# A hybrid decoder layer on one core: the up projection's products reordered, a w_out tile by its other half, embedding products in both pools, triangular products merged

## The chip, the cores and the metric

The kernel runs on one core of one Trainium2 chip. The metric is the device time of one execution in microseconds (us). A time "of a kernel" is the median over several executions; a profile is of one execution, whose own time is given beside it. TensorE is called PE here and its weight loads PEld; VectorE is DVE, ScalarE is ACT, GpSimd is POOL, SyncE is SP.

## The reference

One decoder layer on x of 512 tokens by 1024 features, all in fp32. Cut to the parts that the change touches:

```python
# stick-breaking attention, per head: s < t
z = einsum('bhqd,bhkd->bhqk', qi, kt) * scale
log_keep = where(before, log_sigmoid(-z), 0)
later = cumsum(log_keep, axis=3, reverse=True) - log_keep
a = where(before, exp(log_sigmoid(z) + later), 0)
...
merged = g0 * (o_da @ w_branch_da) + g1 * (o_sb @ w_branch_sb) + g2 * (o_dl @ w_branch_dil)
x = layer_norm(ALPHA * x + merged @ w_out)
...
h = square(relu(x @ w_up))                        # 1024 -> 4096
x = layer_norm(ALPHA * x + h @ w_down + sigmoid(x @ w_g) * (p @ w_ple))
```

The remaining parts (input projection, differential and dilated attention, the three branch projections) are the same in both kernels.

## The kernel before

**Precision.** Each fp32 operand is split into a rounded part and a remainder ("h" and "l": `wh`, `wl`, `x1hT`, `x1lT`, `mh`, `ml`). A product is then three matmuls that add into one bank of the accumulator memory (PSUM): h by h, h by l, l by h. Lines L87 to L89 (`mm3`) are these three for the input projection and the up projection; L887 to L889 are the three of w_out, L955 to L957 those of the embedding, L1017 to L1019 those of its gate. ACT makes the rounded part of a weight chunk (cast at L243, 128x1024), DVE the remainder (L245, `wl<-raw,wh`).

**PSUM.** There are eight banks of 128x512, in two pools that each hand out their banks in rotation: `mm_bank` has two, `at_bank` six. A bank is handed out again only when the readers of its previous content are done.

**Items.** From the input projection on, the program is a list of items. Each names the weight chunks that it needs, a bank, a function `mm` that issues the products and a function `ev` that issues the evacuation (the copy or sum that reads the bank); `ev` of an item is called just before `mm` of the next. An item with no bank of its own takes one of `mm_bank`. Weight chunks are loaded by SP's queue (`raw`), in the order in which `chunk` was called, and cast in the same order, a ring ahead of the items that use them. Sums of weight blocks (`usum`, `dsum`) are made ahead of time by accumulating transfers on POOL's queue. The order of the calls is not altogether the order on an engine: some products of a neighbouring item are moved forward or back when the program is built.

**Stages**, by the first and last weight load in the trace: the heads of the stick-breaking attention put their triangular products (L1666) between other work from 29.7 to 217.9 us; w_out (`wout_items`) runs from 607.4 to 657.3, the embedding (`ple_items`) from 658.0, its gate (`pleg_items`, L1017) from 672.2 to 709.5, and the MLP from there to the end.

**Up projection.** The 4096 hidden features are in eight blocks `m`. A block is 2x2 halves of the weights by 2x2 quarters of x and is computed in Strassen's manner, with seven block products instead of eight; `forms[p]` are the needed sums of quarters of x. A block has two tiles `j` of 128 features each, and a tile four parts, so the items of a block run a0, a1, b0, b1, c0, c1, e0, e1 (`up_parts`, `pair`). Every product here is 128x256, and a block product of a tile is four steps of three matmuls, so 12 of them. Part a has two block products: the one with weight quarter "12", which is called the *second product* below, into the upper half (`HC`) of a bank, and the one with "11", the *first product*, into the lower half (`HB`). Between them ACT copies the second product out to a tile `up` (L1195). The first product remains in the bank, which parts b, c and e use on. Part a's `ev` adds the lower half and the copy into `hid`. L1229 is the last reader of the bank, in part e.

From block 1 on the items of the down projection (`down_parts`, L1261 to L1263, 128x512) of the block before are put between those of up parts, a fixed share after each up part from the third on in a stage; stages hold blocks 0; 1 and 2; 3 and 4; 5 and 6; 7.

**w_out.** Output tile `tt` (four of them, times two halves of the columns) sums eight k steps over `merged_T`, the transposed and split merged rows. `turn_item` makes these: eight transposes (L794), ACT's rounding to `mh` (L798), DVE's remainder `ml`. In the first half of the columns, two turn items follow tile 0 and two more tile 1; those behind tile 1 make k steps 0 to 3 of tiles 2 and 3, those behind tile 0 their k steps 4 to 7.

**Embedding.** Eight products p·w_ple of 6 matmuls each, in `at_bank`; ACT copies each to a tile `ple` (L961). Between them stand the transposes of the normalised rows (L924, `ln1_gen`), in `at_bank` as well, whose readers are ACT's `x1hT` and `x1r` (L937) and DVE's `x1lT` (L931).

**Triangular products.** Per head, the suffix sums within a key block are products of `tri_r` with the split log terms `sph` and `spl`. Key blocks 2 and 3 are two halves of one bank (number 2, 256 columns each), and their terms are two halves of one tile.

Of the kernel before, what the change touches and what calls it, by code (L numbers as in the profile page):

```python
# [55 lines left out]
def trunk(tc, a, out):  # L56
    nc = tc.nc
    es = ExitStack()
    with es:
# [14 lines left out]
        def slot(name, dt=F32):  # L74
            return big.tile([P, 512], dt, name=nm(name), tag="s", bufs=NSLOT)
# [4 lines left out]
        def mm_bank():  # L80
            return psum.tile([P, 512], F32, name=nm("mm"), tag="mm", bufs=2)
# [184 lines left out]
        def item(cs, mm, ev, need=None, bank=None, size=1.0):  # L266
            items.append({"c": cs, "mm": mm, "ev": ev, "need": need, "bank": bank, "size": size})
# [93 lines left out]
        HB = slice(0, 256)  # L361
        HC = slice(256, 512)
# [514 lines left out]
        def wout_items():  # L877
            for half in range(2):
                cs = [chunk(a["wo"][half, c].rearrange("p k n -> p (k n)"), 1024) for c in range(4)]
                for tt in range(4):  # L880
                    def mm(ps, tt=tt, cs=cs):
                        for k in range(8):
                            c = cs[k // 2]
                            s = slice((k % 2) * 512, (k % 2) * 512 + 512)
                            h, lo = merged_T[k // 4, tt // 2, k % 4 // 2]
                            q = slice(k % 2 * 256 + tt % 2 * P, k % 2 * 256 + tt % 2 * P + P)
                            nc.tensor.matmul(ps, h[:, q], c["h"][:, s], start=k == 0, stop=False)  # L887
                            nc.tensor.matmul(ps, h[:, q], c["l"][:, s], start=False, stop=False)
                            nc.tensor.matmul(ps, lo[:, q], c["h"][:, s], start=False, stop=k == 7)  # L889

                    def ev(ps, tt=tt, half=half):
                        y = xn.pop((tt, half))
                        if not half:
                            x1sum[tt] = small("lsm", 2)
                        i = nc.vector.scalar_tensor_tensor(y, y, ALPHA, ps, op0=OP.mult, op1=OP.add,
                                                           accum_out=x1sum[tt][:, half:half + 1])
                        st["added"] = getattr(i, "ins", i)
                        x1[tt, half] = y
                        if half:
                            pending.append(ln1_gen(tt))  # L900
                    item(cs if tt == 3 else [], mm, ev, need=cs, bank=at_bank)
                    for t in {0: [(1, 1, 0), (1, 1, 1)], 1: [(0, 1, 0), (0, 1, 1)]}.get(tt, ()) if not half else ():
                        turn_item(*t)
# [41 lines left out]
        def ple_items():  # L945
            cs = [chunk(a["wp"][half].rearrange("p k n -> p (k n)"), 1024) for half in range(2)]
            for half in range(2):
                for tt in range(4):
                    def mm(ps, tt=tt, half=half):
                        c = cs[half]  # L950
                        for k in range(2):
                            s = slice(k * 512, k * 512 + 512)
                            q = slice(tt * P, tt * P + P)
                            h, lo = pTs[k]
                            nc.tensor.matmul(ps, h[:, q], c["h"][:, s], start=k == 0, stop=False)  # L955
                            nc.tensor.matmul(ps, h[:, q], c["l"][:, s], start=False, stop=False)
                            nc.tensor.matmul(ps, lo[:, q], c["h"][:, s], start=False, stop=k == 1)  # L957

                    def ev(ps, tt=tt, half=half):
                        t = slot("ple")  # L960
                        nc.scalar.copy(t, ps)  # L961
                        ple[tt, half] = t
                    item([cs[half]] if tt == 3 else [], mm, ev, need=cs, bank=at_bank)


        sums_first = set()
# [158 lines left out]
        hid = {}  # L1125
# [33 lines left out]
        def up_parts(m):  # L1159

            cs = {}
            wu = a["wu"][m]

            def operand(n):
                src = usum[m][n] if isinstance(n, int) else wu[{"11": 0, "12": 1, "21": 2, "22": 3}[n]].rearrange(
                    "p k n -> p (k n)")
                cs[n] = chunk(src, 1024)

            def pair(j):
                js = slice(256 * j, 256 * j + 256)  # L1170
                b = {}

                def prod(ps, p, n, start, stop):
                    c = cs[n]
                    for k in range(4):
                        s = slice(512 * j + k * P, 512 * j + k * P + P)
                        mm3(ps, c["h"][:, s], c["l"][:, s], *forms[p][k], start and k == 0, stop and k == 3)

                def bank(n, new):
                    def f():  # L1180
                        b[n] = new()
                        return b[n]
                    return f

                def add(need, mm, ev, bank):
                    if j == 0:
                        for n in need:
                            operand(n)
                    item([cs[n] for n in need] if j else [], mm, ev, need=[cs[n] for n in need], bank=bank)

                def part_a():
                    def mm(ps):
                        prod(ps[:, HC], 2, "12", True, True)
                        b["s"] = slot("up")
                        nc.scalar.copy(b["s"][:, HB], ps[:, HC])  # L1195
                        prod(ps[:, HB], 1, "11", True, False)

                    def ev(ps):
                        if j == 0:
                            hid[m] = [slot("hid") for _ in range(4)]  # L1200
                        nc.vector.tensor_add(hid[m][0][:, js], ps[:, HB], b["s"][:, HB])
                    add(("12", "11"), mm, ev, bank("x", mm_bank))

                def part_b():
                    def mm(ps):
                        prod(ps[:, HB], 7, 2, True, False)
                        prod(b["x"][:, HB], 6, 1, False, False)

                    def ev(ps):
                        nc.scalar.copy(b["s"][:, HC], b["x"][:, HB])  # L1210
                        nc.scalar.copy(b["s"][:, HB], ps[:, HB])
                    add((2, 1), mm, ev, bank("y", at_bank))

                def part_c():
                    def mm(ps):
                        prod(ps[:, HB], 5, 0, False, False)

                    def ev(ps):
                        nc.vector.tensor_add(hid[m][3][:, js], ps[:, HB], b["s"][:, HB])
                    add((0,), mm, ev, lambda: b["x"])  # L1220

                def part_e():
                    def mm(ps):
                        prod(b["x"][:, HB], 3, 3, False, True)
                        prod(ps[:, HB], 4, "22", False, True)

                    def ev(ps):
                        nc.vector.tensor_add(hid[m][1][:, js], ps[:, HB], b["s"][:, HC])
                        nc.scalar.activation(hid[m][2][:, js], b["x"][:, HB], AF.Relu)  # L1229
                        if j:  # L1230
                            for n, sign in ((0, 1.0), (2, 0.0), (1, -1.0), (3, -1.0)):
                                if sign:
                                    nc.scalar.activation(hid[m][n], hid[m][n], AF.Relu, scale=sign)
                                nc.scalar.activation(hid[m][n], hid[m][n], AF.Square)
                    add((3, "22"), mm, ev, lambda: b["y"])
                return [part_a, part_b, part_c, part_e]
            return [x for y in zip(pair(0), pair(1)) for x in y]

# [218 lines left out]
        tri_r = one.tile([P, P], F32R, name="tri_r")  # L1457
# [151 lines left out]
        def sb_head(hd):  # L1609
# [5 lines left out]
            bank = [at_bank() for _ in range(3)]  # L1615
            for kb, bi, c0, n in reversed(blk):
                m = mask_b.rearrange("p a b -> p (a b)") if kb == 3 else mask_b[:, 1, :]
# [43 lines left out]
                yield  # L1661
            ah, al = {}, {}
            for kb, bi, c0, n in reversed(blk):
                ps = bank[bi][:, c0:c0 + n]
                for hl in (sph, spl):
                    nc.tensor.matmul(ps, tri_r, hl[bi][:, c0:c0 + n], start=False, stop=False, skip_group_check=True)  # L1666
                if kb < 3:
                    n2, hl = later[kb]
                    for t in hl:
# [488 lines left out]
```

## Time and profile before

| | |
|---|---|
| median of 3 runs | 1039.94 us (1039.53 to 1040.59) |
| profiled execution, its own time | 1040.08 us |
| its span, first to last instruction | 1038.1 us |
| mean granted clock of PE | 0.998 |
| instructions | 15050 |
| DMA moved | 249.21 MB, mean 240 GB/s |

The span is what the rows of the trace cover; the execution's own time is 2.0 us longer. In rows of the trace the first column is the start in us from the span's beginning (or a window), the second the time that the row's instructions took, then engine, line, operation, output and inputs; "x8" stands for eight in a row that were folded together. A bracket at the end is the time for which the engine was idle before it, and what ended that. A line's number is that of the kernel before.

### The profile page before, as it was taken

To read this page: it belongs to the slowest core of one execution; us is meant where nothing else is said; L and a number is where in the kernel's file an instruction comes from. 1 tells how busy PE (TensorE), PEld (TensorE's weight loads), DVE (VectorE), ACT (ScalarE), POOL (GpSimd) and SP (SyncE) were. 2 spreads that over 40 slices of the span, in tenths; PEclk is the share of its full clock that TensorE was granted. 3 is DMA by queue.
4 is the path that set the end of the run, shared out by engine and by line. 5 is a ranking of instruction groups with operands and counts; after the bars stand their busy time and mean duration, and the time that the engine had idled before them with its cause. 6 is when DMAs were issued, how large, how long until landed. Compare 5 with 4: busy or idle time off the path is not lost.

```text
span 1038.1 us, 15050 instructions
## 1 busy us (share of the span) xinstructions
PE 1028.0 (99%) x5448; PEld 881.2 (85%) x5448; DVE 787.0 (76%) x1412; ACT 591.7 (57%) x1010; POOL 180.1 (17%) x271
## 2 busy tenths in 40 slices
PE   9999999999999999999999999999999999999997
PEld 6888888889888888888888888889999889889886
DVE  6888667769765657779688885798768877877965
ACT  7566544536434645676675743775666556555651
POOL 0002411120211232411011040111111111111001
PEclk9999999999999999999999999999999999999999
DMA  8449968485976999977789795579999999998612
GB/s 309 121 156 271 277 193 217 120 290 144 285 182 222 271 272 294 238 205 199 227 269 235 267 320 182 160 222 319 331 290 315 301 306 340 303 295 279 235 57 81
DMA packets 71322, 249.21 MB, mean 240 GB/s; under 512 B 8808, under 2 KB 9592, under 8 KB 71248
## 3 DMA queue, kind: packets, MB, share of 16 engines
q0 software_dynamic: 32464, 116.21, 44.8%
q1 hardware_dynamic: 38208, 131.13, 35.1%
q8 instruction: 43, 0.70, 0.3%
q10 hardware_dynamic: 576, 0.92, 0.2%
q14 instruction: 31, 0.25, 0.1%
HBM read 246.10 MB, written 98.59 MB: 332 GB/s over the span
## 4 chain that ended last, share of the span: by engine, by line
PE 94%; DVE 2%; ACT 1%; DMA 1%; issue 1%; SPq 0%; POOL 0%; DVEq 0%; ACTq 0%; POOLq 0%
PE mm L87 10%; PE mm L88 10%; PE mm L89 10%; PE at L1261 4%; PE at L1262 4%; PE at L1263 4%; PE at L599 3%; PE at L600 3%; PE at L601 3%; PE mm L496 2%; PE mm L498 2%; PE mm L497 2%; PE at L89 1%; PE at L88 1%; PE at L87 1%; PE at L761 1%
## 5 line engine op out<-in xcount | busy, mean ns | idle before, releaser
L243 ACT CAST wh<-raw 128x1024 fp32r<-128x1024 f32 x257 | 268.6, 1049 | 242.0 <-PE mm L88 134.2
L245 DVE TENSOR_TENSOR wl<-raw,wh 128x1024 fp32r<-128x1024 f32 x257 | 312.7, 1223 | 112.9 <-ACT wh L243 111.3
L87 PE MATMUL mm<-xhT,wh 128*128 128x512 f32 x302 | 119.1, 394 | 0.0
L89 PE MATMUL mm<-xhT,wl 128*128 128x512 f32 x302 | 118.2, 391 | 0.0
L88 PE MATMUL mm<-xlT,wh 128*128 128x512 f32 x302 | 118.1, 391 | 0.0
L1261 PE MATMUL at<-wh,hh 128*128 128x512 f32 x188 | 73.7, 392 | 0.0
L87 PE MATMUL mm<-x1hT,wh 128*128 128x256 f32 x256 | 73.7, 288 | 0.0
L1262 PE MATMUL at<-wl,hh 128*128 128x512 f32 x188 | 73.7, 392 | 0.0
L1263 PE MATMUL at<-wh,hl 128*128 128x512 f32 x188 | 73.1, 389 | 0.0
L88 PE MATMUL mm<-x1lT,wh 128*128 128x256 f32 x256 | 72.2, 283 | 0.0
L89 PE MATMUL mm<-x1hT,wl 128*128 128x256 f32 x256 | 71.8, 283 | 0.0
L89 PEld LDWEIGHTS mm<-xhT,wl 128*128 128x128 f32 x302 | 56.8, 188 | 11.9
L87 PEld LDWEIGHTS mm<-xhT,wh 128*128 128x128 f32 x302 | 56.7, 188 | 11.0
L88 PEld LDWEIGHTS mm<-xlT,wh 128*128 128x128 f32 x302 | 56.7, 188 | 10.8
L87 PEld LDWEIGHTS mm<-x1hT,wh 128*128 128x128 f32 x256 | 48.7, 190 | 4.8 <-ACT up L1195 3.0
L88 PEld LDWEIGHTS mm<-x1lT,wh 128*128 128x128 f32 x256 | 48.8, 191 | 1.5
L89 PEld LDWEIGHTS mm<-x1hT,wl 128*128 128x128 f32 x256 | 48.6, 191 | 0.0
L1095 POOL DMA_DIRECT2D usum<-in_wu_dram x32 | 28.3, 921 | 101.6 <-DMA usum<-usum 34.8
L1095 POOL DMA_DIRECT2D dsum<-in_wd_dram x28 | 25.6, 936 | 102.5 <-DMA dsum<-dsum 37.0
L1263 PEld LDWEIGHTS at<-wh,hl 128*128 128x128 f32 x188 | 35.3, 188 | 7.7
L1261 PEld LDWEIGHTS at<-wh,hh 128*128 128x128 f32 x188 | 35.5, 189 | 6.0
L1262 PEld LDWEIGHTS at<-wl,hh 128*128 128x128 f32 x188 | 35.5, 189 | 5.5
(601 smaller groups left out, 2677.2 us busy)
## 6 DMA issues: line engine op xcount, KB each, us to landing
usum<-in_wu_dram POOLq DMA_DIRECT2D x48, 512.0 KB, 9.0
dsum<-in_wd_dram POOLq DMA_DIRECT2D x42, 512.0 KB, 8.9
raw<-in_wt_dram SPq DMA_DIRECT2D x38, 512.0 KB, 5.1
raw<-usum SPq DMA_DIRECT2D x32, 512.0 KB, 7.7
raw<-dsum SPq DMA_DIRECT2D x28, 512.0 KB, 7.0
raw<-in_wd_dram SPq DMA_DIRECT2D x25, 512.0 KB, 6.1
raw<-in_wu_dram SPq DMA_DIRECT2D x24, 512.0 KB, 7.6
raw<-in_wv_dram SPq DMA_DIRECT2D x18, 512.0 KB, 5.7
```

The costliest lines, as they stand in the source:

```text
L87: nc.tensor.matmul(ps, wh, xh, start=start, stop=False, skip_group_check=True)
L88: nc.tensor.matmul(ps, wh, xl, start=False, stop=False, skip_group_check=True)
L89: nc.tensor.matmul(ps, wl, xh, start=False, stop=stop, skip_group_check=True)
L243: i = nc.scalar.copy(h, raw)
L245: i = nc.vector.tensor_sub(lo, raw, h.bitcast(F32))
L599: nc.tensor.matmul(ps, h[:, q], c["h"][:, n], start=go, stop=False, skip_group_check=True)
L600: nc.tensor.matmul(ps, h[:, q], c["l"][:, n], start=False, stop=False, skip_group_check=True)
L601: nc.tensor.matmul(ps, lo[:, q], c["h"][:, n], start=False, stop=end, skip_group_check=True)
L1095: i = nc.gpsimd.dma_start(o, i, accum_op=OP.add, max_dma_last_dim=4096)
L1261: nc.tensor.matmul(ps, h[:, q], c["h"][:, s], start=go, stop=False, skip_group_check=True)
L1262: nc.tensor.matmul(ps, h[:, q], c["l"][:, s], start=False, stop=False, skip_group_check=True)
L1263: nc.tensor.matmul(ps, lo[:, q], c["h"][:, s], start=False, stop=end, skip_group_check=True)
```

## The change

It has four parts.

**1. Up projection, part a.** The two tiles of a block keep their items a0 and a1, but a0 now issues the second products ("12") of both tiles, each into the upper half of its own `mm_bank` bank and each followed by its copy, and a1 the first products ("11") of both, with the add into `hid` of tile 0 between them and that of tile 1 as its `ev`. Chunk "11" is asked for in a1 instead of a0, so behind the chunks of a down item that stands between the two.

```diff
 def pair(j):
     js = slice(256 * j, 256 * j + 256)
-    b = {}
+    b = both[j]
...
 def part_a():
+    def first(i):
+        nc.vector.tensor_add(hid[m][0][:, 256 * i:256 * i + 256], both[i]["x"][:, HB],
+                             both[i]["s"][:, HB])
+
     def mm(ps):
-        prod(ps[:, HC], 2, "12", True, True)
-        b["s"] = slot("up")
-        nc.scalar.copy(b["s"][:, HB], ps[:, HC])
-        prod(ps[:, HB], 1, "11", True, False)
+        for i in range(2):
+            if j == 0:
+                if i:
+                    both[i]["x"] = mm_bank()
+                x, k = both[i]["x"], "12"
+                prod(x[:, HC], 2, k, True, True, i)
+                both[i]["s"] = slot("up")
+                nc.scalar.copy(both[i]["s"][:, HB], x[:, HC])
+            else:
+                prod(both[i]["x"][:, HB], 1, "11", True, False, i)
+                if not i:
+                    first(i)
 
     def ev(ps):
         if j == 0:
             hid[m] = [slot("hid") for _ in range(4)]
-        nc.vector.tensor_add(hid[m][0][:, js], ps[:, HB], b["s"][:, HB])
-    add(("12", "11"), mm, ev, bank("x", mm_bank))
+        else:
+            first(1)
+    operand(("12", "11")[j])
+    need = [cs[("12", "11")[j]]]
+    item(need, mm, ev, need=need, bank=(lambda: b["x"]) if j else bank("x", mm_bank))
```

PE at part a of block 0. Before, tile 0 is bank `mm_6921` and tile 1 `mm_6955`; `wh_6820` is chunk "12" and `wh_6826` chunk "11":

```order
L87 MATMUL mm_6921<-x1hT,wh_6820 128x256 [waits Activation_49]
...
L89 MATMUL mm_6921<-x1hT,wl_6821 128x256
L87 MATMUL mm_6955<-x1hT,wh_6820 128x256
...
L87 MATMUL mm_6955<-x1hT,wh_6820 128x256
L87 MATMUL mm_6921<-x1hT,wh_6826 128x256 [waits Activation_49]
...
L89 MATMUL mm_6921<-x1hT,wl_6827 128x256
L88 MATMUL mm_6955<-x1lT,wh_6820 128x256
```

The same place after, where tile 0 is `mm_6905`, tile 1 `mm_6920`, chunk "12" `wh_6804` and chunk "11" `wh_6810`:

```order
L87 MATMUL mm_6905<-x1hT,wh_6804 128x256 [waits Activation_49]
...
L89 MATMUL mm_6905<-x1hT,wl_6805 128x256
L87 MATMUL mm_6920<-x1hT,wh_6804 128x256
...
L89 MATMUL mm_6920<-x1hT,wl_6805 128x256
L87 MATMUL mm_6905<-x1hT,wh_6810 128x256 [waits Activation_49]
...
L89 MATMUL mm_6905<-x1hT,wl_6811 128x256
L87 MATMUL mm_6920<-x1hT,wh_6810 128x256 [waits Activation_49]
```

Before, four products of tile 1 stood between tile 0's second and first product; now all 12 do, and tile 1's first product stands behind the 12 of tile 0's.

ACT around the two copies of the last block, before:

```order
L243 CAST wh_9530<-raw_9390 128x1024 [waits DMAHW1_49,PE_49]
L1195 COPY up_9558<-mm_9545 128x256 [waits PE_49]
L243 CAST wh_9604<-raw_9411 128x1024 [waits DMAHW2_49,PE_49]
L1195 COPY up_9590<-mm_9577 128x256 [waits PE_49]
L243 CAST wh_9610<-raw_9417 128x1024 [waits DMAHW3_49,PE_49]
L1211 COPY up_9558<-at_9617 128x256 [waits DVE_49,PE_49]
```

and after:

```order
L243 CAST wh_9514<-raw_9374 128x1024 [waits DMAHW1_49,PE_49]
L1208 COPY up_9542<-mm_9529 128x256 [waits PE_49]
L243 CAST wh_9559<-raw_9395 128x1024 [waits DMAHW2_49,PE_49]
L1208 COPY up_9557<-mm_9544 128x256 [waits PE_49]
L243 CAST wh_9594<-raw_9401 128x1024 [waits DMAHW3_49,PE_49]
L1252 ACTIVATE hid_9565<-hid_9565 128x512 [waits DVE_49]
```

The copies (L1208 is L1195 of before) have a cast between them in both; behind them part b's copy has moved behind the work on `hid`.

**2. w_out.** The third tile of the first half of the columns takes its k steps in the order 4 to 7, 0 to 3.

```diff
+ks = (4, 5, 6, 7, 0, 1, 2, 3) if tt == 2 and not half else range(8)
+
-def mm(ps, tt=tt, cs=cs):
-    for k in range(8):
+def mm(ps, tt=tt, cs=cs, ks=ks):
+    for k in ks:
...
-        nc.tensor.matmul(ps, h[:, q], c["h"][:, s], start=k == 0, stop=False)
+        nc.tensor.matmul(ps, h[:, q], c["h"][:, s], start=k == ks[0], stop=False)
         nc.tensor.matmul(ps, h[:, q], c["l"][:, s], start=False, stop=False)
-        nc.tensor.matmul(ps, lo[:, q], c["h"][:, s], start=False, stop=k == 7)
+        nc.tensor.matmul(ps, lo[:, q], c["h"][:, s], start=False, stop=k == ks[-1])
```

**3. Embedding.** In the first half of the columns, tiles 1 and 3 take a bank of `mm_bank`.

```diff
-item([cs[half]] if tt == 3 else [], mm, ev, need=cs, bank=at_bank)
+item([cs[half]] if tt == 3 else [], mm, ev, need=cs,
+     bank=None if tt % 2 and not half else at_bank)
```

PE's first product of tiles 1 to 3 and of the fifth tile, and the transposes of the next token tile (L924 before, L926 after); before:

```order
L955 MATMUL at_6448<-wh_6217,pTh_6255 128x512 [waits DVE_49,Activation_49]
...
L955 MATMUL at_6469<-wh_6217,pTh_6255 128x512 [waits DVE_49,Activation_49]
...
L955 MATMUL at_6490<-wh_6217,pTh_6255 128x512 [waits DVE_49]
...
L955 MATMUL at_6505<-wh_6223,pTh_6255 128x512 [waits Activation_49]
...
L924 MATMUL at_6514<-ident,xn_5943 128x128 [waits DVE_49,Activation_49]
```

and after:

```order
L957 MATMUL mm_6432<-wh_6201,pTh_6239 128x512 [waits PE_49]
...
L957 MATMUL at_6453<-wh_6201,pTh_6239 128x512 [waits DVE_49,Activation_49]
...
L957 MATMUL mm_6474<-wh_6201,pTh_6239 128x512
...
L957 MATMUL at_6489<-wh_6207,pTh_6239 128x512 [waits DVE_49,Activation_49]
...
L926 MATMUL at_6498<-ident,xn_5927 128x128 [waits DVE_49]
```

Every tile is where it was in the row; two of them no longer take a turn in the rotation of six, so the fifth takes another bank of it.

**4. Triangular products.** The products of key block 2 are left out, and those of key block 3 run over the whole bank: two of 512 columns for four of 256.

```diff
 for kb, bi, c0, n in reversed(blk):
     ps = bank[bi][:, c0:c0 + n]
-    for hl in (sph, spl):
-        nc.tensor.matmul(ps, tri_r, hl[bi][:, c0:c0 + n], start=False, stop=False, skip_group_check=True)
+    for hl in (sph, spl) if kb != 2 else ():
+        nc.tensor.matmul(bank[bi][:, :w[bi]], tri_r, hl[bi], start=False, stop=False,
+                         skip_group_check=True)
```

The rest of the program is unchanged. The order of POOL's instructions is the same; on SP's queue only loads of the MLP change places, as said under part 1.

More of the change, by code (lines that the diff above doesn't have):

```diff
@@ L1161, in up_parts @@
             cs = {}
+            both = [{}, {}]
             wu = a["wu"][m]
@@ L1170, in pair, with prod @@
                 js = slice(256 * j, 256 * j + 256)
-                b = {}
-                def prod(ps, p, n, start, stop):
+                b = both[j]
+                def prod(ps, p, n, start, stop, j=j):
                     c = cs[n]
@@ L1663, in sb_head @@
             for kb, bi, c0, n in reversed(blk):
-                ps = bank[bi][:, c0:c0 + n]
-                for hl in (sph, spl):
-                    nc.tensor.matmul(ps, tri_r, hl[bi][:, c0:c0 + n], start=False, stop=False, skip_group_check=True)
+                for hl in (sph, spl) if kb != 2 else ():
+                    nc.tensor.matmul(bank[bi][:, :w[bi]], tri_r, hl[bi], start=False, stop=False,
+                                     skip_group_check=True)
                 if kb < 3:
```

## The prediction

> **What bounds the kernel now.** I read the busy table first, then the chain of waits, then who waited for whom on PE's weight loads (PEld). Matmuls are pipelined, so a stalled PE still shows as busy; the start times of successive weight loads show a stall better.
>
> ```profile
> PE 1028.0 (99%) x5448; PEld 881.2 (85%) x5448; DVE 787.0 (76%) x1412; ACT 591.7 (57%) x1010; POOL 180.1 (17%) x271
> PE 94%; DVE 2%; ACT 1%; DMA 1%; issue 1%; SPq 0%; POOL 0%; DVEq 0%; ACTq 0%; POOLq 0%
> PEld mm L87 <- ACT up L1195: 3.0, 13, 0.3
> PEld at L955 <- ACT ple L961: 0.6, 1, 0.6
> PEld at L887 <- ACT mh L798: 0.5, 1, 0.5
> ```
>
> PE is the bound from end to end: 99% busy and 94% of the chain. So only two things help: PE waits that disappear, or PE work that disappears. Three of the few waits PE has are where this change edits: the copy of a second product in the up projection (3.0 us in 13 pieces), one embedding product (0.6) and the third w_out tile (0.5). That is a ceiling of 4.1 us, and what an idle time is worth has to be read from the loads around it.
>
> **Up projection, what one wait costs.** Part a computes a tile's second product into the upper half of a bank, ACT copies it out (L1195), and the first product goes into the lower half of the same bank. PE waits for the copy. The first of the 16 waits, and its copy:
>
> ```profile
> 712.05 0.19 PEld L87 LDWEIGHTS mm<-x1hT,wh 128*128 128x128 f32 x1
> 712.48 0.19 PEld L87 LDWEIGHTS mm<-x1hT,wh 128*128 128x128 f32 x1 [0.23 <-ACT up L1195]
> 712.70 0.19 PEld L89 LDWEIGHTS mm<-x1hT,wl 128*128 128x128 f32 x1
> 712.06 0.36 ACT L1195 COPY up<-mm 128x256 f32<-128x256 f32 x1
> ```
>
> The last of the 16, with the cast and copy ahead of it on ACT:
>
> ```profile
> 954.36 0.19 PEld L87 LDWEIGHTS at<-t7h,wh 128*128 128x128 f32 x1
> 954.48 0.19 PEld L88 LDWEIGHTS at<-t7l,wh 128*128 128x128 f32 x1
> 955.56 0.19 PEld L88 LDWEIGHTS at<-t7l,wh 128*128 128x128 f32 x1
> 955.92 0.19 PEld L87 LDWEIGHTS mm<-x1hT,wh 128*128 128x128 f32 x1 [0.18 <-ACT up L1195]
> 956.15 0.19 PEld L89 LDWEIGHTS mm<-x1hT,wl 128*128 128x128 f32 x1
> 954.55 1.05 ACT L243 CAST wh<-raw 128x1024 fp32r<-128x1024 f32 x1 [2.50 <-PE mm L88]
> 955.51 0.37 ACT L1195 COPY up<-mm 128x256 f32<-128x256 f32 x1
> ```
>
> Undisturbed loads of 256-wide products are 0.12 us apart (954.36 to 954.48). From 712.05 three loads take 0.65 instead of 0.36: price 0.29, the shown idle and 0.06. From 955.56 they take 0.59: price 0.23. Ten of the 16 waits stand behind 256-wide products; their idles, read from the timeline, sum to 1.67, with 0.055 each 2.22. The other six stand behind 512-wide down products, where the load has room of its own:
>
> ```profile
> 836.24 0.19 PEld L1262 LDWEIGHTS at<-wl,hh 128*128 128x128 f32 x1
> 836.47 0.19 PEld L1263 LDWEIGHTS at<-wh,hl 128*128 128x128 f32 x1
> 836.99 0.19 PEld L87 LDWEIGHTS mm<-x1hT,wh 128*128 128x128 f32 x1 [0.33 <-ACT up L1195]
> 837.22 0.19 PEld L89 LDWEIGHTS mm<-x1hT,wl 128*128 128x128 f32 x1
> ```
>
> A 512-wide product takes 0.23, so 836.47 to 837.22 should have been 0.23 + 0.23 + 0.12 = 0.58 and was 0.75: price 0.17, the idle less 0.16. The six together are 0.65. All 16: **2.87 us**.
>
> **What the new order leaves.** The first tile's copy now has the other tile's 12 products over it: 1.44 us against about 0.43 (712.05 to 712.48). That wait goes in all eight blocks. The second tile's copy has only the first tile's first product over it wherever no down part stands between the two items. That is so in blocks 0, 1, 3, 5 and 7. And there ACT has a cast between the two copies, into the buffer that the 12 products themselves free. The last wait quoted is this same row of events: the tile's products end, t7 begins at 954.36, the cast starts 0.19 later, the copy follows, and PE gets on at 955.92, 1.56 after 954.36. Before, 11 products lay over it; now 12, so 0.12 is gained and 0.11 stays. Block 0, whose wait cost 0.28, keeps 0.16. So 0.11 × 4 + 0.16, with rounding 0.6, stays, and the net is **2.25** (bounds 0, if other waits take their place, and 2.87).
>
> Tile 1's second product now starts 12 products into the block and needs its bank, which ACT empties at the end of the block before:
>
> ```profile
> 730.78 0.38 ACT L1229 ACTIVATE hid<-mm 128x256 f32<-128x256 f32 x1
> 732.51 0.19 PEld L87 LDWEIGHTS mm<-x1hT,wh 128*128 128x128 f32 x1
> ```
>
> That is the tightest place, block 1, where no down part stands between the blocks: free at 731.16, needed at 732.51. The old order had fillers there that already needed this bank, so the row shows the new case too: 1.35 to spare, price nothing; if ACT came 2 us late it would cost 0.65. DVE's adds come one item later than before but still 24 products (2.9 us) ahead of the product that reuses the bank.
>
> **w_out.** The third tile began with the half of the merged rows that had just been transposed and waited for ACT to round it:
>
> ```profile
> 622.97 1.02 PEld L794 LDWEIGHTS mm<-ident,b 128*128 128x128 f32 x8
> 624.47 0.19 PEld L887 LDWEIGHTS at<-wh,mh 128*128 128x128 f32 x1 [0.48 <-ACT mh L798]
> 624.80 0.19 PEld L887 LDWEIGHTS at<-wh,mh 128*128 128x128 f32 x1
> 623.83 1.07 ACT L798 CAST mh<-mm 128x512 fp32r<-128x512 f32 x2 [4.19 <-PE mm L794]
> 651.60 1.03 PEld L924 LDWEIGHTS at<-ident,xn 128*128 128x128 f32 x8
> 652.94 0.19 PEld L889 LDWEIGHTS at<-wh,ml 128*128 128x128 f32 x1
> ```
>
> From eight transposes to the third load behind them an undisturbed place takes 652.94 - 651.60 = 1.34; here 624.80 - 622.97 = 1.83. Price 0.49. The other half was rounded before, and its 12 products (2.7 us) cover the casts that end at 624.90 and the subtractions behind them. All of **0.49** goes; what comes after it starts from PE's w_out products, so it moves along. Bounds 0 and 0.49.
>
> **Embedding.** The fifth product took the bank of the first one, whose copy ACT had queued behind layer norm work:
>
> ```profile
> 664.07 0.19 PEld L957 LDWEIGHTS at<-wh,pTl 128*128 128x128 f32 x1
> 665.24 0.19 PEld L957 LDWEIGHTS at<-wh,pTl 128*128 128x128 f32 x1
> 664.28 0.56 ACT L961 COPY ple<-at 128x512 f32<-128x512 f32 x1
> 671.18 1.02 PEld L924 LDWEIGHTS at<-ident,xn 128*128 128x128 f32 x8
> 672.17 0.19 PEld L1017 LDWEIGHTS at<-wh,x1hT 128*128 128x128 f32 x1
> 670.51 0.68 DVE L931 TENSOR_TENSOR x1lT<-at,x1hT 128x512 fp32r<-128x512 f32 x1
> 671.23 0.65 ACT L937 COPY x1r<-at 128x256 f32<-128x256 f32 x2 [0.65 <-DVE x1lT L931]
> ```
>
> Three loads took 1.17 instead of 3 × 0.23 = 0.68: price 0.49. With two products in the other pool, the fifth takes a bank emptied long before. But the wait has a successor. Counting six banks on, the first gate product (672.17) takes the bank of the third token tile's second transposes, before and after alike, and its last reader is that L937 pair, done at 671.88, 671.94 with the 0.06 a release takes (712.42 to 712.48). That reader hangs on DVE's and ACT's own queues, not on PE. PE would arrive 0.49 earlier, at 671.68, and wait 0.26. So **0.23** stays; bounds 0 and 0.49. The Trainium skill (PSUM — Partial Sum Buffer, PSUM bank collisions raise a hardware error) says that no two engines may use one bank and quadrant together, reads against reads included; the trace agrees, since L937 waits 0.65 for DVE's read of the same transposes. Without that order between readers the copies could have run earlier and the whole 0.49 would be gained.
>
> **Triangular products.** Per head four 256-wide products become two 512-wide ones on the same columns.
>
> ```profile
> 62.52 0.19 PEld L1666 LDWEIGHTS at<-spl,tri_r 128*128 128x128 f32 x1
> 62.64 0.19 PEld L1666 LDWEIGHTS at<-sph,tri_r 128*128 128x128 f32 x1
> ```
>
> 4 × 0.12 against 2 × 0.227 saves 0.027, over eight heads **0.21**; a few products in the first two heads also change places with projection products, which I take as nothing (bounds ±0.3). By the Trainium skill (TensorE: Matmul & The Clock Gate, Back-to-back issue gap) a matmul costs its columns and a fixed 2.5 ns; 16 fewer would then save an estimated 0.04 us, and the sum would be 0.17 smaller. The 13 ns that these rows show per product decide it for me.
>
> **The sum.** 2.25 + 0.49 + 0.23 + 0.21 = 3.18. The profiled execution took 1040.08 (span 1038.1 and 2.0 around it), so 1036.90; its runs' median is 0.14 lower, so **1036.8 us**.
>
> **The rivals.** *Everything goes* (0.2): ACT and DVE run ahead, and neither the second copies nor the gate product wait. 2.87 + 0.49 + 0.49 + 0.21 = 4.06, 1035.9. Against it: the cast between the copies is tied to PE itself.
>
> *The up projection's waits come back* (0.17): the copy behind the cast, or a bank, holds PE as long as before, in nearly all blocks. Then 0.93 is left, 1039.0. For it: ACT already has 57% and casts of 1.05 that hold the queue. Against it: blocks 2, 4 and 6 have down products of 1.4 us and more in between.
>
> *Slower: late weights* (0.07). The loads for the up projection's second operand are now requested one item later, behind those of the down parts, while the DMA engines are full:
>
> ```profile
> 790.00:880.00 90.00, 90.00 (x587) 81.88 (x587) 68.95 (x88) 54.57 (x84) 14.03 (x22) 1.00 1.00 313
> raw<-usum SPq DMA_DIRECT2D x32, 512.0 KB, 7.7
> ```
>
> The first row's last three columns are clock, DMA share and GB/s: share 1.00. If a block's operand came so late that PE sees its cast and subtraction (1.05 and 1.23), the three blocks with down parts in between would lose 6.8, against 3.2 gained: 1043.5. It decides once landing takes longer than the cover, six buffers of 24 × 0.12 = 2.9 us, 17 us against the 7.7 shown. No PE wait in the up projection names a cast or a load, which speaks against it.
>
> *It doesn't do what it says* (0.06): a scheduler sets the order, and could have put the same products back between. The order shows it did not in the up blocks, but other shifts could eat the gain: 1039.9.
>
> **How the numbers follow.** My forecast has 0.5, with its own range 1036.0 to 1037.8. A measurement of this kernel tells about 0.2%, 2.1 us, from no change: faster is below 1037.9, slower above 1042.0. The forecast (nearly all), the first rival, and half of the second, which would stop halfway, give 0.77; the rest of it and the fourth 0.16; late weights 0.07. The range: below to the first rival with 0.4 for the spread of the runs, 1035.5; above to the second rival, 1039.0. That leaves out the slower case and little more.
>
> **What would show it.** Right: of the 13 waits on the up copy about five are left, each under 0.1 of idle, all at second tiles without a down part ahead; no wait on mh at the third w_out tile; no wait on ple, but one of about 0.26 on x1r at the first gate product; 16 fewer products at the triangle line. Wrong: up waits of 0.2 in all blocks, PE waits on L1229 or on adds of DVE, or PE waiting on wl or raw between 710 and 960.

## The result, and the profile after

The change takes 1037.71 us (median of 12 runs, 1036.98 to 1038.59) where the kernel before took 1040.39 beside it (12 runs, 1039.53 to 1040.92): 2.7 us less, a ratio of 0.9975 with an interval of 0.9967 to 0.9984. The profiled execution took 1037.69 us, with a span of 1035.7. The busy table and the chain of the page of the change:

```profile
PE 1025.8 (99%) x5432; PEld 880.7 (85%) x5432; DVE 786.2 (76%) x1412; ACT 592.5 (57%) x1010; POOL 180.6 (17%) x271
PE 96%; DVE 2%; ACT 1%; DMA 0%; issue 0%; DVEq 0%
L87 PEld LDWEIGHTS mm<-x1hT,wh 128*128 128x128 f32 x256 | 48.9, 191 | 1.9
raw<-in_wu_dram SPq DMA_DIRECT2D x24, 512.0 KB, 7.5
```

PE is still the bound, with 16 products fewer. The idle time ahead of the up projection's first weight load of a step fell from 4.8 to 1.9 us, and the up copy is no longer named. On the page of the kernel before this row was

```profile
L87 PEld LDWEIGHTS mm<-x1hT,wh 128*128 128x128 f32 x256 | 48.7, 190 | 4.8 <-ACT up L1195 3.0
```

Loads of up weights land as fast as before (7.5 against 7.6 us).

Where the time went is best read between landmarks that both programs have: the first mask product of the third head, the first product with the fold matrix, the first of w_out, the embedding, the up projection and the last down stage. The view by windows, cut at these, before (window, its length, then busy times of PE, PEld, DVE, ACT, POOL):

```profile
70.13:243.45 173.32, 173.24 (x842) 146.04 (x842) 127.53 (x238) 86.78 (x140) 39.31 (x60) 1.00 0.77 219
607.36:657.96 50.60, 50.36 (x237) 41.45 (x236) 34.78 (x62) 18.57 (x32) 8.20 (x15) 1.00 0.60 197
657.96:710.15 52.19, 51.98 (x242) 42.97 (x240) 48.01 (x70) 39.89 (x69) 8.16 (x12) 1.00 0.82 254
710.15:997.62 287.47, 287.42 (x1886) 262.50 (x1885) 222.87 (x287) 179.14 (x276) 40.61 (x60) 1.00 0.93 293
```

and of the change:

```profile
70.43:243.95 173.52, 173.43 (x831) 145.45 (x830) 127.90 (x238) 86.99 (x140) 39.63 (x60) 1.00 0.77 219
607.92:658.04 50.12, 50.12 (x238) 41.44 (x236) 34.82 (x62) 18.56 (x32) 8.24 (x15) 1.00 0.59 199
658.04:710.00 51.96, 51.96 (x242) 43.05 (x240) 47.78 (x69) 39.68 (x69) 7.64 (x11) 1.00 0.82 250
710.00:995.21 285.21, 285.21 (x1886) 262.76 (x1885) 221.94 (x287) 180.04 (x276) 41.27 (x61) 1.00 0.93 296
```

The up projection's stretch is 2.26 us shorter, w_out's 0.48, the embedding and its gate's 0.23. The heads 3 to 8 are 0.20 *longer*. That sums to 2.77 less. The remaining 0.36 of the difference to the spans' 2.4 lies at the start (the third head begins at 70.43 instead of 70.13) and in the stretch from 243 to 607 us (0.06). The three kernels below that leave the heads as they were begin the third head at 69.76, 70.06 and 70.23, so 0.3 at the start is chance of an execution.

The places that the prediction named, in the change. The second tile's copy of blocks 0 and 7 (lines 1208 and 243 are its copy and the cast ahead of it):

```profile
713.22 1.05 ACT L243 CAST wh<-raw 128x1024 fp32r<-128x1024 f32 x1 [0.94 <-ACT up L1208]
714.18 0.36 ACT L1208 COPY up<-mm 128x256 f32<-128x256 f32 x1
714.30 0.19 PEld L89 LDWEIGHTS mm<-x1hT,wl 128*128 128x128 f32 x1
714.59 0.19 PEld L87 LDWEIGHTS mm<-x1hT,wh 128*128 128x128 f32 x1
951.78 0.37 ACT L1208 COPY up<-mm 128x256 f32<-128x256 f32 x1
951.95 0.19 PEld L89 LDWEIGHTS mm<-x1hT,wl 128*128 128x128 f32 x1
952.20 0.19 PEld L87 LDWEIGHTS mm<-x1hT,wh 128*128 128x128 f32 x1
```

Two loads are 0.29 and 0.25 apart where undisturbed ones are 0.12: a rest of 0.17 and 0.13, with an idle time of only 0.10 and 0.06, so small that the list of waits doesn't name it. The same gap stands at the second tiles of blocks 1, 3 and 5 (0.25, 0.24, 0.24) and at no other part a. The load behind a gap comes a little earlier than usual. Over two intervals, as the prediction measured its prices, block 0 has 0.40 for 0.24 (714.30 to 714.70) and the four others 0.35 to 0.36, so the rests are 0.16 and four times 0.11 to 0.12, together 0.62. The other two places:

```profile
623.58 1.02 PEld L794 LDWEIGHTS mm<-ident,b 128*128 128x128 f32 x8
624.58 0.19 PEld L889 LDWEIGHTS at<-wh,mh 128*128 128x128 f32 x1
624.92 0.19 PEld L891 LDWEIGHTS at<-wh,ml 128*128 128x128 f32 x1
664.15 0.19 PEld L959 LDWEIGHTS mm<-wh,pTl 128*128 128x128 f32 x1
664.38 0.19 PEld L957 LDWEIGHTS at<-wh,pTh 128*128 128x128 f32 x1
672.00 0.19 PEld L1020 LDWEIGHTS at<-wh,x1hT 128*128 128x128 f32 x1 [0.24 <-ACT x1r L939]
671.31 0.65 ACT L939 COPY x1r<-at 128x256 f32<-128x256 f32 x2 [0.66 <-DVE x1lT L933]
```

From eight transposes to the third w_out load it is now 1.34, and the fifth embedding product follows at the usual 0.23. The first gate product waits 0.24 for the x1r copy, a wait that the kernel before did not have.

### The profile page after: what moved, and what is told of

Same layout as the page of the kernel before. It is cut to its first block, busy times and chain, and to the rows that moved or that the text cites. A ratio compares the mean times of both kernels' runs of the same rounds, so it can differ in the third digit from the quotient of the medians.

```text
span 1035.7 us, 15013 instructions
## 1 busy us (share of the span) xinstructions
PE 1025.8 (99%) x5432; PEld 880.7 (85%) x5432; DVE 786.2 (76%) x1412; ACT 592.5 (57%) x1010; POOL 180.6 (17%) x271
## 4 chain that ended last, share of the span: by engine, by line
PE 96%; DVE 2%; ACT 1%; DMA 0%; issue 0%; DVEq 0%
PE mm L87 10%; PE mm L88 10%; PE mm L89 10%; PE at L1280 4%; PE at L1281 4%; PE at L1282 4%; PE at L599 3%; PE at L601 3%; PE at L600 3%; PE mm L496 2%; PE mm L498 2%; PE mm L497 2%; PE at L89 1%; PE at L88 1%; PE at L87 1%; PE at L891 1%
```

## The experiments

Each kernel was timed beside the kernel before on one chip; the times of short stretches come from its profiled execution.

### The change without the merge, and the merge alone

`no_tri` is the change with these lines of the kernel before:

```diff
-for hl in (sph, spl) if kb != 2 else ():
-    nc.tensor.matmul(bank[bi][:, :w[bi]], tri_r, hl[bi], start=False, stop=False, skip_group_check=True)
+ps = bank[bi][:, c0:c0 + n]
+for hl in (sph, spl):
+    nc.tensor.matmul(ps, tri_r, hl[bi][:, c0:c0 + n], start=False, stop=False, skip_group_check=True)
```

> The change without its fourth part (triangular products left as four of 256 columns per head). Theory A (the merge costs: the profile of the change was 0.20 us later at the end of heads 3 to 8 than at their start, where before it was not, and 0.11 in the first two heads): the stretch from the first mask product of the third head to the first fold product goes back from 173.52 to 173.32 us, and the whole is 0.2 to 0.4 us faster than the change, 1037.3 to 1037.5 us. Rival B (the drift is chance of one execution): the stretch is anywhere in 173.3 to 173.55 whatever the products are, and the whole is the change's own 1037.7. Rival C (the merge saves the 0.21 that was forecast, and something else in the change lost 0.4): the whole is 0.2 slower, 1037.9.

`tri_only` is the kernel before with the opposite edit and nothing else.

> The kernel before with the fourth part alone. Theory A (the merge costs about 0.04 us in each of the later heads): heads 3 to 8 take 173.52 instead of 173.32 us, and the whole is 0.2 to 0.3 us slower than before. Rival C (it saves 0.027 per head): 173.15 and 0.2 faster than before. In no case more than 0.5 either way. The products behind the merged ones tell the mechanism: by A the nine or ten 512-column products that follow take 0.232 us each instead of 0.227.

`no_tri` took 1036.98 us (8 runs), ratio 0.9971 (0.9961 to 0.9981); `tri_only` 1040.45 (11 runs), ratio 1.0006 (0.9998 to 1.0015). The kernel before beside both: 1039.99. The windows of heads 3 to 8, first of `no_tri`, then of `tri_only`:

```profile
70.23:243.55 173.32, 173.24 (x842) 146.04 (x841) 127.54 (x238) 86.97 (x140) 39.67 (x60) 1.00 0.77 219
```

```profile
70.17:243.68 173.51, 173.43 (x830) 145.43 (x829) 128.09 (x238) 87.14 (x140) 39.49 (x60) 1.00 0.77 219
```

The stretch is 173.32 without the merge and 173.51 with it, whatever else is changed: theory A. The medians point the same way (without the merge 3.01 less than the kernel before beside it, where the change has 2.68; the merge alone 0.46 more), by somewhat more than the stretch explains, but 0.2 us is at the limit of what the times can tell. Chance (rival B) is out, since the stretch repeats to 0.01: 173.32 or 173.33 in the four kernels here without the merge and with the ones last, 173.51 or 173.52 in the four with the merge. Where it is lost shows in one head, from the first triangular load to the next mask product; the kernel before:

```profile
114.05 0.19 PEld L1666 LDWEIGHTS at<-sph,tri_r 128*128 128x128 f32 x1
114.28 0.19 PEld L1666 LDWEIGHTS at<-spl,tri_r 128*128 128x128 f32 x1
114.87 0.19 PEld L87 LDWEIGHTS mm<-xhT,wh 128*128 128x128 f32 x1
117.71 0.28 PEld L1618 LDWEIGHTS <-identb 128*128 128x128 bf16 x4 [0.26 <-issue]
```

and the change:

```profile
114.34 0.19 PEld L1684 LDWEIGHTS at<-sph,tri_r 128*128 128x128 f32 x1
114.57 0.19 PEld L1684 LDWEIGHTS at<-spl,tri_r 128*128 128x128 f32 x1
115.15 0.19 PEld L87 LDWEIGHTS mm<-xhT,wh 128*128 128x128 f32 x1
118.05 0.22 PEld L1637 LDWEIGHTS <-identb 128*128 128x128 bf16 x3 [0.26 <-issue]
```

The spacing of the loads lags by one product: in both kernels the second load stands 0.23 behind the first, the length of the long product ahead of the group. The group itself went from 0.82 to 0.81. The 12 products of the projection behind it, which nobody touched, went from 2.84 to 2.90. That repeats in each of the four heads that have such a stretch (2.84 each before, 2.90, 2.90, 2.90 and 2.89 after).

### The up projection alone

`up_only`: the kernel before with the first part of the change.

> The kernel before with the first part alone. Theory (the first copies are hidden by 12 products, five second copies leave 0.11 to 0.16 each): 2.25 us less than before, 1038.1 where before is 1040.4; no wait over 0.2 us of PE on the up copy; in blocks 0, 1, 3, 5 and 7 two loads at the second tile's first product stand 0.23 to 0.28 apart instead of 0.12. Rival (the waits of the whole part vanish): 2.87 less. Rival (the gain of the whole change was from the other parts): under 1 us less.

It took 1037.70 us (10 runs), 2.29 less than before, ratio 0.9979 (0.9970 to 0.9989). Its window from the first up product to the last down stage:

```profile
709.92:995.13 285.21, 285.21 (x1886) 262.75 (x1885) 221.83 (x287) 180.00 (x276) 41.17 (x61) 1.00 0.94 296
```

2.26 less than the 287.47 of before, to the hundredth what the whole change has there. The gaps at the second tiles are the expected ones, 0.29 in block 0 and 0.24 in blocks 1, 3, 5 and 7, and no wait on the up copy is named. Neither rival holds.

### w_out and embedding alone

`wout_ple`: the kernel before with the second and third part.

> The kernel before with the second and third part alone. Theory (0.49 from w_out, 0.49 from the embedding of which a wait of 0.26 on the x1r copy at the first gate product takes back about half): 0.7 us less than before. Rival (the gate's wait takes all of what both bring, since its reader hangs on DVE and ACT alone): the first gate product starts where it did, 0 less. Rival (both whole): 1.0 less and no wait at the gate.

It took 1039.21 us (11 runs), 0.78 less, ratio 0.9993 (0.9985 to 1.0002), so the time alone hardly tells it from no change. Its windows do:

```profile
607.24:657.32 50.08, 50.08 (x238) 41.45 (x237) 34.80 (x62) 18.57 (x32) 8.22 (x15) 1.00 0.62 201
657.32:709.27 51.95, 51.95 (x242) 43.05 (x241) 47.77 (x69) 39.66 (x69) 7.62 (x11) 1.00 0.81 247
```

0.52 less in w_out and 0.24 less in the embedding with its gate. The gate takes back about half of what the embedding's products gain, as expected, and none of w_out's.

### The gate's bank

`gate_bank`: the change with

```diff
 if p in (1, 2, 7):
-    b[name, r] = at_bank()
+    b[name, r] = mm_bank() if p == 2 else at_bank()
```

> The change with the first two gate products of the embedding (the ones called z) in banks of the two-bank pool instead of the six-bank pool. Theory (the first gate product waits 0.24 us for the x1r copy only because it takes the bank of those transposes): the wait at the first gate product is gone and the whole is 0.24 us faster than the change, 1037.5. Rival (what follows inherits it: the next gate product takes the same bank 2.7 us later, when it is free, or the up projection's first bank waits for the gate's reader): no change, or a new wait at the up projection's first product.

It took 1037.41 us (12 runs; ratio 0.9976, 0.9967 to 0.9984; before 1040.05). The difference to the change is below what the times tell; the windows and the two rows at the gate:

```profile
658.16:709.83 51.67, 51.67 (x242) 43.04 (x240) 47.49 (x69) 39.67 (x69) 7.64 (x11) 1.00 0.81 247
709.83:995.05 285.22, 285.22 (x1886) 262.79 (x1884) 222.15 (x287) 180.07 (x276) 41.30 (x61) 1.00 0.94 297
```

```profile
670.86 1.02 PEld L926 LDWEIGHTS at<-ident,xn 128*128 128x128 f32 x8
671.85 0.19 PEld L1020 LDWEIGHTS mm<-wh,x1hT 128*128 128x128 f32 x1
```

The wait is gone, 0.29 of the stretch with it, and the up projection behind inherits nothing. So the wait was the bank's, as the prediction had it.

### The second copy on DVE

`copy_dve`: the change with

```diff
-nc.scalar.copy(both[i]["s"][:, HB], x[:, HC])
+(nc.vector.tensor_copy if i else nc.scalar.copy)(both[i]["s"][:, HB], x[:, HC])
```

> The change with the second tile's copy in part a on DVE instead of ACT. Theory (what is left of the up waits is the cast ahead of that copy on ACT, 0.11 to 0.17 in five blocks): the doubled gap between two loads at the second tile's first product goes in the blocks where DVE is idle at that time, and up to 0.6 us less than the change, 1037.1. Rival (DVE's weight remainders of 1.23 us hold the copy longer than the cast did): new waits of up to 1 us in some blocks, and a slower kernel, up to 1040. Rival (the gap is a property of the switch from 12 products of one tile to the other's, whoever copies): no change, and the gaps stay at 0.23 to 0.28.

It took 1037.07 us (6 runs; ratio 0.9970, 0.9959 to 0.9981; before 1040.05). Its window of the MLP, and the rows of block 0:

```profile
709.58:994.47 284.89, 284.89 (x1886) 262.59 (x1884) 224.40 (x295) 177.89 (x268) 41.25 (x61) 1.00 0.93 296
```

```profile
710.92 2.35 DVE L245 TENSOR_TENSOR wl<-raw,wh 128x1024 fp32r<-128x1024 f32 x2
713.19 0.69 DVE L990 SCALAR_TENSOR_TENSOR xn<-xn,sg 128x512 f32<-128x512 f32 x1
713.79 0.42 DVE L1208 COPY up<-mm 128x256 f32<-128x256 f32 x1
713.88 0.19 PEld L89 LDWEIGHTS mm<-x1hT,wl 128*128 128x128 f32 x1
714.26 0.19 PEld L87 LDWEIGHTS mm<-x1hT,wh 128*128 128x128 f32 x1 [0.18 <-DVE up L1208]
```

The same place in block 1:

```profile
733.37 0.42 DVE L1208 COPY up<-mm 128x256 f32<-128x256 f32 x1 [0.25 <-PE mm L89]
734.37 0.19 PEld L89 LDWEIGHTS mm<-x1hT,wl 128*128 128x128 f32 x1
734.49 0.19 PEld L87 LDWEIGHTS mm<-x1hT,wh 128*128 128x128 f32 x1
```

In blocks 1, 3, 5 and 7 the gap is gone: in block 1 DVE is idle until PE is done and copies at once, where in the change the copy stood in ACT's queue behind the cast (733.58 to 734.63, the copy from 734.54). So the cast ahead of the copy was the cause. In block 0, where the copy stands behind two weight remainders and a sum (L990) in DVE's queue, the gap grew from 0.29 to 0.38. The stretch is 0.32 shorter; four rests of 0.12 less 0.09 would be 0.39, so some of it did not reach the end.

### The order of the short products

`ones_first`: the change with the products of `ones_r` issued ahead of the triangular ones in each key block (the sums are the same).

```diff
-for hl in (sph, spl) if kb != 2 else ():
-    nc.tensor.matmul(bank[bi][:, :w[bi]], tri_r, hl[bi], ...)
-if kb < 3:
-    n2, hl = later[kb]
-    for t in hl:
-        nc.tensor.matmul(bank[bi][:, c0 + n - n2:c0 + n], ones_r, t, ...)
 if kb == 3:
     continue
+n2, hl = later[kb]
+for t in hl:
+    nc.tensor.matmul(bank[bi][:, c0 + n - n2:c0 + n], ones_r, t, ...)
+for hl in (sph, spl):
+    nc.tensor.matmul(bank[bi][:, :w[bi]], tri_r, hl[bi], ...)
```

> The change with the products of ones issued ahead of the triangular products in each key block, so that no short products stand between the merged 512-column ones and the projection's. Theory A2 (the projection's products run slower after the switch from two short products back to long ones): the nine or ten long products after the merged ones take 0.227 us again and heads 3 to 8 take 173.2 to 173.3 us instead of 173.52. Rival (the slower pace belongs to the merged products themselves or to something beside them): 173.5 as in the change. The whole within 0.4 us of the change in any case.

1037.27 us (5 runs; ratio 0.9971, 0.9959 to 0.9983). The window of heads 3 to 8:

```profile
70.24:243.33 173.09, 173.01 (x830) 145.35 (x829) 127.76 (x238) 86.95 (x140) 39.65 (x60) 1.00 0.77 219
```

0.43 less than in the change, more than the theory's 0.22 to 0.32. The loads of the long products behind the merged ones stand 0.23 apart at first and then 0.227 again, as theory A2 expected. Its reason, the switch from two short products back to long ones, cannot be the whole of it: here too the two products of ones stand between long products, those of the projection ahead of them and the merged ones behind, and the slow pace does not come. To split the 0.43, `ones_first_no_tri` has the same order without the merge:

> The change with the triangular products unmerged (four of 256 columns in the bank of key blocks 2 and 3) and the products of ones ahead of the triangular ones in each key block. It splits the 0.43 us that the order with ones first gained over the change (heads 3 to 8: 173.09 against 173.52; unmerged in the old order 173.32). Theory O (the order alone does it, the merge is worth nothing): 173.1. Theory M (the gain of the order lies in the merged products no longer being followed by two short ones, and without the merge the order is worth only what the middle group showed, 0.03 a head): 173.2 to 173.3.

One execution took 1037.19 us. Its heads 3 to 8, from the first mask load at 70.27 to the first fold load at 243.43, take 173.16. So 0.16 comes from the order alone: the middle group of a head (eight products of key blocks 0 and 1) goes from 1.47 to 1.41, of which the work behind it gives 0.03 back. Theory M had named these 0.03 a head, but neither theory gave the stretch. The merge can now be read in both orders: with the two products of ones behind, it costs 0.20 in six heads (173.32 to 173.52); with them ahead, it saves 0.07 (173.16 to 173.09).

Two kernels merge only one of the two operands. `four_short` has a merged product, then two of 256 columns and the two of ones; `two_short` has two of 256, then the merged one, then those of ones:

```diff
-for hl in (sph, spl) if kb != 2 else ():
-    nc.tensor.matmul(bank[bi][:, :w[bi]], tri_r, hl[bi], ...)
+whole = [(sph, 0, 512), (spl, 256, 256), (spl, 0, 256)] if kb == 3 else [] if kb == 2 else [(sph, c0, n), (spl, c0, n)]
+for hl, o, m in whole:
+    nc.tensor.matmul(bank[bi][:, o:o + m], tri_r, hl[bi][:, o:o + m], ...)
```

(`two_short` has `(sph, 256, 256), (sph, 0, 256), (spl, 0, 512)` there.)

> The change with only the first of the two triangular operands merged: one product of 512 columns, then two of 256, then the two of ones, so four short products stand ahead of the projection's long ones where the change has two and the kernel before six. In the runs so far the 12 projection products behind this group take 2.84 us after six short ones, 2.90 after two, and 2.95 with the first of them 0.12 later after none. Theory S (the pace of the long products depends on how many short ones stand right ahead of them): 2.84 to 2.87. Rival M (it is a matter of any merged 512-column product in the group): 2.90.

> The change with only the second of the two triangular operands merged: two products of 256 columns, then one of 512, then the two of ones. Theory S (only the number of short products right ahead counts): 2.90 us for the 12 projection products behind, as in the change. Rival T (all short products of the group count, four here): 2.84 to 2.87. The whole of both kernels within 0.3 us of the change.

One execution of each: 1039.11 and 1037.19 us, with spans of 1035.3 and 1035.2. The first time stands 3.8 over its span where the others have 2.0, so only the traces are read. Their windows of heads 3 to 8, `four_short` first:

```profile
70.30:243.69 173.39, 173.31 (x836) 145.78 (x836) 127.82 (x238) 86.96 (x140) 39.09 (x60) 1.00 0.77 219
```

```profile
70.11:243.55 173.44, 173.35 (x836) 145.76 (x835) 128.06 (x238) 86.98 (x140) 39.49 (x60) 1.00 0.76 219
```

The 12 products behind the group took 2.86 in all four heads of the first, 2.87 or 2.88 in those of the second. That is between 2.84 (none merged) and 2.90 (both). The first lies in theory S's range and is not rival M's 2.90; the second is below S's 2.90 and at or just above the top of what rival T wanted, so no theory gives both. Over the six heads one merged product costs 0.07 (173.39 against 173.32) when it stands first and 0.12 (173.44) when it stands right ahead of the products of ones, where both cost 0.20. All slowed kernels have a merged product somewhere ahead of the two products of ones; why that slows the products behind is not settled by these runs.

### The amendments together

`best`: the change with ones ahead, the gate's bank and the second copy on DVE in all blocks but the first (`if i and m`).

> The change with three amendments together: products of ones ahead of the triangular ones, the first two gate products in the two-bank pool, the second tile's copy on DVE in all blocks but the first. Theory (they are in stages apart and add up): 0.43 less in heads 3 to 8, 0.27 less at the gate, 0.4 less in the up projection, so 1.1 us less than the change and 3.5 to 3.8 less than before, 1036.4. Rival (one of them shifts the others' order): the stretches differ from 173.09, 13.69 and 284.8.

1036.69 us (7 runs, 1035.78 to 1037.53; before 1039.97), ratio 0.9967 (0.9956 to 0.9979), so 3.3 less than before, a little short of the 3.5 to 3.8 expected; its profiled execution took 1036.15. Its windows:

```profile
70.13:243.20 173.07, 173.01 (x830) 145.33 (x829) 127.78 (x239) 86.97 (x140) 39.44 (x60) 1.00 0.77 219
607.10:657.22 50.12, 50.12 (x238) 41.45 (x237) 34.82 (x62) 18.57 (x32) 8.23 (x15) 1.00 0.60 195
657.22:708.89 51.67, 51.67 (x242) 43.04 (x240) 47.49 (x69) 39.66 (x69) 7.64 (x11) 1.00 0.82 250
708.89:993.71 284.82, 284.82 (x1886) 262.57 (x1884) 224.46 (x294) 178.20 (x269) 41.15 (x61) 1.00 0.94 296
```

Against the change: 0.45, 0, 0.29 and 0.39 less, 1.13 in all. The three add up. By its interval the whole is clearly below the kernel before; against the change the intervals overlap, and it is the stretches that speak for it.

## Why the prediction was right, and where it was not

The forecast was 3.14 us less than the 1039.94 shown, 1036.8; measured were 2.68 less than the 1040.39 of the kernel before beside it. The 1037.71 lies just inside the forecast's own range. Half of the 0.9 us between 1036.8 and 1037.71 is that the kernel before itself read 0.45 higher, and most of the rest is one term.

- **Up projection, 2.25.** Measured 2.26, alone and within the change. All first copies are hidden, and the five second copies that should leave a rest left it, in just the blocks 0, 1, 3, 5 and 7: gaps of 0.29, 0.25, 0.24, 0.24 and 0.25 instead of 0.12, which by the prediction's own measure leave 0.62 where 0.6 was said. That the cast ahead of the copy causes them was argued from the order of ACT; the DVE copy showed it for four of the five. The bank was never waited for, nor any late weight.
- **w_out, 0.49.** Measured 0.48 in the change and 0.52 beside the embedding alone. The casts are covered.
- **Embedding, 0.23.** Measured 0.23. The successor wait came at the place named, on the reader named, at 0.24 for 0.26. The gate's bank showed that it is the bank. By the order between readers of one bank that the prediction took from the Trainium skill (PSUM — Partial Sum Buffer, PSUM bank collisions raise a hardware error) the copy could not have come earlier; the trace still agrees, since the same copies wait 0.66 for DVE's read.
- **Triangular products, 0.21.** This step failed, in sign. "4 × 0.12 against 2 × 0.227" priced the group by itself and took the products behind it as unchanged. The group gained 0.01 rather than 0.027 a head: the four short loads take 0.47 (114.28 to 114.75) where 4 × 0.12 was said, the two merged ones 0.46 (114.57 to 115.03) where 2 × 0.227 was said, so two small roundings ate half of a small difference. And the 12 products behind it lost 0.06. In the third head the stretch gained 0.01, in each of the five others it lost 0.04: 0.20 more in six heads, not 0.16 less; the first two heads are within the chance of the start. The bounds of ±0.3 were meant for products that change places, and they do not hold it either: 0.21 less 0.3 is a loss of 0.09. That the whole stayed within the range rests on the other three terms, which came out to within 0.01. By the rule of the Trainium skill that the prediction weighed (TensorE: Matmul & The Clock Gate, Back-to-back issue gap; 2.5 ns for each matmul saved) two fewer products a head save an estimated 0.005; with the products of ones ahead the runs show 0.07 in six heads, 0.012 a head, between that and the 0.027.

Of the rivals, "everything goes" needed the second copies and the gate to be free, which they were not; "the waits come back" and "late weights" did not happen at all. "Other shifts could eat the gain" is what the fourth part did, with 0.20 of it.

## What to carry to other kernels

A wait that is removed by reordering leaves whatever stands second in the queue of the engine that released it: look there, and at the bank or buffer that the work ahead of it now reaches earlier, and price both; here both came within 0.1 us. Short idle times are not named in the list of waits (in the kernel before, of the 16 waits on the up copy, those of 0.17 and more were named, and those of 0.14 and 0.10 were not), so read the spacing of successive weight loads against an undisturbed place. A saving of a few products is not finished with the products themselves: compare the time from one landmark to the next in both programs, since the pace of untouched work behind can take more than was saved.

## What the runs showed of the hardware that was not expected

Long products run at a pace that depends on what stood ahead of them: with the two products of ones last in the group, the 12 loads behind it took 2.84 us when all four triangular products were short, 2.86 to 2.88 with one merged, 2.90 with both, at the same granted clock (1.00) and with as many instructions on the other engines. With the ones ahead and both merged it was 2.95, of which 0.12 is only that the last product of the group is then a long one, so the pace was the old one. The cause stays open. Stretches between landmarks repeat far better than whole times: heads 3 to 8 took 173.32 or 173.33 in four kernels without the merge and 173.51 or 173.52 in four with it, all with the products of ones last, while whole times of one kernel spread by over 1 us.
